# adaLN weights in one buffer of their own: blocks of 384 columns, eight k-tiles multiplied in one piece

## The chip, the cores and the metric

The kernel runs on one core of a Trainium2 chip. The metric is the device time of one execution in microseconds; smaller is better.

## The reference, cut to what matters

Two layers work on 256 context and 256 latent tokens of width 1024. Each layer first turns the two conditions into six modulation vectors of 1024 entries; two of them shift, two scale and two gate:

```python
mod_l = (silu_c @ ada_w[layer] + ada_b[layer])[:, None, :]
mod_c = (silu_cc @ ada_w[layer] + ada_b[layer])[None, None, :]
sh1_l, sc1_l, g1_l, sh2_l, sc2_l, g2_l = jnp.split(mod_l, 6, axis=-1)
...
h_l = rms_norm(xl, norm1_g[layer]) * (1.0 + sc1_l) + sh1_l
proj = jnp.concatenate([h_c, h_l], axis=1) @ w_in[layer]
...
xl = xl + g1_l * (jnp.concatenate([a_l, b_l, g_l], axis=-1) @ w_out[layer])
h2_l = rms_norm(xl, norm2_g[layer]) * (1.0 + sc2_l) + sh2_l
...
xl = xl + g2_l * y[:, y.shape[1] - n_lat:]
```

`proj` feeds three groups of heads (A: differential attention, B: windowed attention, C: gated linear attention). `y` is a SwiGLU in layer 0 (the FFN) and a choice of two out of eight experts in layer 1. `ada_w` is [2, 1024, 6144] in float32: per layer 48 blocks of 128 columns, eight blocks for each of the six vectors.

## The kernel before, in words

**Stages.** On TensorE the program runs: the projection of layer 0 with groups C, A and B; the output projection; the FFN in two halves of 1408 hidden columns; the same mixing for the latent tokens of layer 1; router and experts. Weights are loaded in float32 and split by ScalarE (high part, line 219) and VectorE (low part, line 385), and a product is three matmuls (lines 645 to 647).

**What sets the order.** Until the experts, all work is added as pieces to `Plan` (line 89): an engine, an estimated time, what it comes after, a rank, and the rings of buffers that it takes and gives back. `Plan.run` plays the list through once, on the host: whenever an engine is free, the first in rank of the pieces that can start goes next. What it finds is the order in which each engine's queue is written, DMA issues included; all the loads named here stand in SyncE's queue (SP). On the chip each queue runs strictly in that order.

**adaLN.** `ada` (line 421) makes one unit for `nb` blocks of 128 columns. It loads the columns of all eight k-tiles (line 431), into two halves or one buffer. `products` (line 442) multiplies four k-tiles at a time, each in its own 32 columns of the array, in two pieces of work; the second adds to the sums of the first. ScalarE copies the result (`adar`), TensorE transposes it block by block (`adat`, line 452), and VectorE adds the four rows and the bias into `mods` (lines 456 and 457). The buffer counts as free for the planner when the copy is done; on the chip the next load waits for the products alone.

**Where the units stand.** The first 16 blocks of layer 0 come at the start of the program, in buffers of the ring `long`. Blocks 16 to 41 are 13 units of two blocks in layer 0's attention, in the two buffers of the ring `raw`, through which all weights go as well. Blocks 42 to 47 and layer 1's blocks 0 to 31 are 13 units of three blocks (the last of two) in the FFN, in the two buffers `mixC`. Layer 1's blocks 32 to 47 are 8 units of two blocks in layer 1's attention, in `raw` again. The units of the attention have a rank behind everything else there: they fill.

**Around them.** Attention runs in units: scores (`sA`, `sB`, lines 1219 to 1221), exponentials (ScalarE, line 1231) on maxima by VectorE (line 1236), transposes (`pT`, line 1241), products with the values (`oAp`, `oBp`). The scores read `qmA`, the queries by groups in a tile that is zero elsewhere: GpSimd clears it (line 1190), ScalarE and VectorE write its high and low parts. `out_C` (weights `oCw`, line 1405) is group C's part of the output projection, in eight pieces of nine matmuls `oCp`; a piece needs its entry of the gate `g1`, and VectorE adds the result onto the tokens (line 653). It too fills the attention.

Of the kernel before, what the change touches and what calls it, by code (L numbers as in the profile page):

```python
# [11 lines left out]
F32 = mybir.dt.float32  # L12
# [7 lines left out]
PSUM = bass.MemoryType.PSUM  # L20
# [7 lines left out]
EPS = 1e-6  # L28
# [60 lines left out]
class Plan:  # L89
    """Pieces of work for the engines, issued in an order found by list scheduling: whenever an engine is free, the first  # L90
    in rank of the pieces whose needs are met and whose memory is free."""
# [8 lines left out]
    def add(self, engine, us, f, after=(), rank=0.0, take=(), give=(), order=()):  # L100
        """take, give: names of rings, a buffer each; taken at the start, given back at the end. order: names of
        sequences that the piece continues"""
# [6 lines left out]
    def release(self, after, rings):  # L109
        """gives memory back when the pieces are done"""  # L110
        return self.add("none", 0.0, lambda: None, after, 0.0, (), rings)
# [61 lines left out]
def trunk(ctx: ExitStack, tc: tile.TileContext, A, out, dbg=None):  # L173
    nc = tc.nc
# [23 lines left out]
    def acc4(n=4, kind=None):  # L198
        """accumulators of one product group: half of PSUM, one pair of banks and two single ones, or of one kind"""
# [25 lines left out]
    # ---------------- constants and small parameters  # L225
# [16 lines left out]
    # ---------------- tokens, feature-major  # L242
# [4 lines left out]
    def rsqrt_steps(get, scale, nm):  # L247
        """1 / sqrt(src * scale + EPS), with one Newton step, in pieces for DVE, ACT, DVE; get() returns dst, src"""
# [29 lines left out]
    plan = Plan(big=2, sm=4, hi=2, lo=2, raw=2, sp=2, work=10, long=24, mixC=2, b16=2, units=5, oC=2)  # L278
    add = plan.add

    # ---------------- tokens, feature-major, and the small parameters
# [9 lines left out]
    def start():  # L291
        """Returns the pieces after which silu(c), silu(c_ctx), the other small parameters and the tokens with their sums
        of squares are there."""
# [41 lines left out]
        # silu(c), silu(c_ctx) as the first two of 32 columns  # L335
# [38 lines left out]
    def parts(make, n, after, rank, take=(), give=(), order=()):  # L374
        """high and low parts of n columns; make() returns a list of (high, low, source). Returns the two pieces of work."""
# [14 lines left out]
    class Weights:  # L390
        """k-tiles of weights: load() returns the raw ones, views() the places of the high and low parts, pieces(self, k)
        a k-tile's (high, low, source)"""
# [21 lines left out]
    def w_load(src, segs, hk):  # L414
        """load of columns segs of src's k-tiles 4 hk .. 4 hk + 3, and its time"""
        return lambda: w_cols(src, segs, hk), 0.00146 * 4 * sum(n for _, n in segs)

    # ---------------- adaLN modulation, feature-major: mods[l][p, section*8 + k, (lat, ctx)]
    mods = [consts.tile([128, 48, 2], F32, name=f"mods{l}") for l in range(2)]

    def ada(l, b0, nb, rings, rank, after=()):
        """nb blocks of 128 columns from block b0 on; a column group of the array for each k-tile of four"""
# [4 lines left out]
        for i, r in enumerate(rings):  # L427
            def load(i=i, r=r):
                t = (KT(nm="idle") if r == "long" else k2.tile([128, 1536], F32, name="idle", tag=r, bufs=2) if r == "mixC" else
                     ring.tile([128, 2048], F32, name="idle", tag=r, bufs=2))[:, :per * n].rearrange("p (k f) -> p k f", k=per)  # L430
# [28 lines left out]
        a = add("PE", n * 0.002, lambda: products(0), [loads[(len(rings) - 1) // 2], have_c], rank, ["sm"])  # L459
        a = add("PE", n * 0.002, lambda: products(1), [a, *have], rank)  # L460
# [9 lines left out]
    def amul(l, sec, g, nm):  # L470
        """g * (1 + scale) of section sec, k-tiles lo..hi - 1 at a time."""
# [8 lines left out]
    def split(dst_hi, dst_lo, src, pieces=1):  # L480
        """pieces: along the first free dimension"""
# [7 lines left out]
    # ---------------- norm + modulation, feature-major  # L489

    def squares(k, t0, t1, after, rank, place=None):
        """squares of x^T's k-tile into the running sum (the last k-tile's stay apart); place: for the sum, where it outlasts
        this part"""
# [139 lines left out]
    def w_cols(src, segs, hk):  # L633
# [3 lines left out]
        o = 0  # L637
# [1728 lines left out]
```

## Time and profile before

| | |
|---|---|
| median of 3 runs | 1944.68 us (1943.29 to 1944.72) |
| profiled execution | span 1941.8 us; the page gives no other time of it |
| TensorE (PE) busy | 1904.0 us, 98% of the span |
| VectorE (DVE) busy | 1427.7 us, 74% |
| ScalarE (ACT) busy | 1170.6 us, 60% |
| adaLN products on PE | 57.1 us, 42 units |
| chain that ended last | PE 94%, DMA 2%, DVE 2%, ACT 1% |

Times in the trace count from the start of the span. A timeline row gives the start of its group, how long it was busy, engine, line, operation, output<-inputs, shapes and how many; in brackets the idle time of the engine just before it. Matmuls overlap, so the time that one takes from its engine is read from start to start. A float32 matmul of `adap` leaves two records. A window row gives for each engine its busy time and how many instructions, then the clock that was granted to PE (1.00 is 2.4 GHz), the busy share of the DMA engines, and GB/s.

### The profile page before, as it was taken

What the parts mean: (1) busy time and instruction counts of PE and PEld (TensorE: products, weight loads), DVE (VectorE), ACT (ScalarE), POOL (GpSimd) and SP (SyncE); (2) the same over time, 40 slices, a digit from 0 to 9 for tenths busy, and PEclk for the clock granted to TensorE, in tenths of its full rate; (3) what the DMA queues carried; (4) which work ended last, traced back from release to release, by engine and by line L of the source; (5) the groups of instructions that cost most, each with busy time, mean ns of one, the idle gap of its engine ahead of it and who ended that gap; (6) DMA issues with size and microseconds to landing.
All of it is one profiled execution on the core that took longest, in us unless ns stands there. A gap on an engine that the chain in (4) does not pass through costs nothing.

```text
span 1941.8 us, 27786 instructions
## 1 busy us (share of the span) xinstructions
PE 1904.0 (98%) x10317; PEld 1562.8 (80%) x10317; DVE 1427.7 (74%) x2330; ACT 1170.6 (60%) x1938; POOL 38.9 (2%) x44
## 2 busy tenths in 40 slices
PE   7999999999999999999999999999999999999998
PEld 4988678877787799887788888888888888888886
DVE  5564987433333345768889998999989999899997
ACT  4443684332222334448777777777777777777776
POOL 1001100000000000020000000000000000000000
PEclk9999999999999999999999999999999999999999
DMA  9313532435434423257799999999999999999991
GB/s 301 102 55 100 182 104 84 155 131 190 141 121 140 148 73 97 83 161 238 281 353 369 363 371 332 356 364 370 373 333 354 372 365 376 327 358 373 373 367 36
DMA packets 268911, 474.41 MB, mean 244 GB/s; under 512 B 14440, under 2 KB 75584, under 8 KB 268640
## 3 DMA queue, kind: packets, MB, share of 16 engines
q1 hardware_dynamic: 268384, 472.37, 69.6%
q8 instruction: 83, 1.36, 0.3%
q0 software_dynamic: 384, 0.19, 0.1%
q14 instruction: 60, 0.49, 0.1%
HBM read 471.47 MB, written 1.05 MB: 243 GB/s over the span
## 4 chain that ended last, share of the span: by engine, by line
PE 94%; DMA 2%; DVE 2%; ACT 1%; issue 0%; SPq 0%; DVEq 0%; ACTq 0%
PE gu L2110 32%; PE py L2135 16%; PE acc L645 9%; PE acc L647 8%; PE acc L646 8%; PE adap L442 2%; PE acc L855 2%; DMA idle<-in_ada_w 2%; PE acc L857 2%; PE acc L856 2%; PE pT L1241 1%; PE mtp L2124 1%; PE oBp L1329 1%; PE gth L2020 1%; PE sct L2159 1%; PE poC L1074 1%
## 5 line engine op out<-in xcount | busy, mean ns | idle before, releaser
L1845 DVE TENSOR_TENSOR mlo<-early,mhi 128x512 fp32r<-128x512 f32 (+1 forms) x350 | 340.0, 1019 | 24.6 <-issue 18.3
L219 ACT ACTIVATE mhi<-early 128x512 fp32r<-128x512 f32 (+1 forms) x352 | 291.3, 885 | 49.0 <-PE py L2135 25.1
L385 DVE TENSOR_TENSOR wlo<-raw,whi 128x512 fp32r<-128x512 f32 (+4 forms) x292 | 150.5, 564 | 157.8 <-ACT whi L219 157.0
L2110 PE MATMUL gu<-mlo,xh 128*128 128x512 f32 x896 | 247.9, 395 | 0.0
L219 ACT ACTIVATE whi<-raw 128x512 fp32r<-128x512 f32 (+4 forms) x292 | 134.9, 525 | 181.5 <-PE acc L646 146.5
L2110 PE MATMUL gu<-mhi,xh 128*128 128x512 f32 x896 | 244.0, 391 | 0.0
L2110 PE MATMUL gu<-mhi,xl 128*128 128x512 f32 x896 | 243.1, 390 | 0.0
L2135 PE MATMUL py<-mhi,hid 128*128 128x512 f32 x896 | 235.3, 390 | 0.0
L645 PE MATMUL acc<-hhi,whi 128*128 128x512 f32 (+1 forms) x576 | 217.6, 378 | 2.8 <-DVE rC L885 1.9
L646 PE MATMUL acc<-hlo,whi 128*128 128x512 f32 (+1 forms) x576 | 210.7, 366 | 2.2 <-DVE hlo L579 2.2
L647 PE MATMUL acc<-hhi,wlo 128*128 128x512 f32 (+1 forms) x576 | 210.6, 366 | 0.5 <-DVE wlo L385 0.5
L1845 DVE TENSOR_TENSOR mlo<-more,mhi 128x1024 fp32r<-128x1024 f32 (+1 forms) x174 | 198.5, 1184 | 11.9 <-issue 10.6
L2110 PEld LDWEIGHTS gu<-mhi,xl 128*128 128x128 f32 x896 | 168.2, 188 | 35.9
L2135 PEld LDWEIGHTS py<-mhi,hid 128*128 128x128 f32 x896 | 167.7, 188 | 35.6
L2110 PEld LDWEIGHTS gu<-mhi,xh 128*128 128x128 f32 x896 | 167.4, 188 | 34.4
L2110 PEld LDWEIGHTS gu<-mlo,xh 128*128 128x128 f32 x896 | 164.4, 188 | 31.5
L219 ACT ACTIVATE mhi<-more 128x1024 fp32r<-128x1024 f32 (+1 forms) x174 | 169.0, 1022 | 28.2 <-PE py L2135 28.2
L1845 DVE TENSOR_TENSOR mlo<-mraw,mhi 128x1024 fp32r<-128x1024 f32 (+1 forms) x116 | 132.5, 1186 | 15.6 <-ACT mhi L219 8.5
L1845 DVE TENSOR_TENSOR mlo<-spare,mhi 128x1024 fp32r<-128x1024 f32 x108 | 127.3, 1220 | 15.3 <-PE py L2135 8.0
L645 PEld LDWEIGHTS acc<-hhi,whi 128*128 128x128 f32 x576 | 108.8, 189 | 35.3 <-issue 11.2
L646 PEld LDWEIGHTS acc<-hlo,whi 128*128 128x128 f32 x576 | 108.9, 189 | 18.9 <-DVE hlo L579 3.1
L647 PEld LDWEIGHTS acc<-hhi,wlo 128*128 128x128 f32 x576 | 108.7, 189 | 18.7 <-DVE wlo L385 0.9
(371 smaller groups left out, 3035.2 us busy)
## 6 DMA issues: line engine op xcount, KB each, us to landing
early<-in_moe_w_up SPq DMA_DIRECT2D x56, 1024.0 KB, 6.0
more<-in_moe_w_up SPq DMA_DIRECT2D x54, 1024.0 KB, 6.2
early<-in_moe_w_gate SPq DMA_DIRECT2D x52, 1024.0 KB, 6.5
spare<-in_moe_w_down SPq DMA_DIRECT2D x48, 1024.0 KB, 6.0
early<-in_moe_w_down SPq DMA_DIRECT2D x112, 256.0 KB, 6.1
mraw<-in_moe_w_gate SPq DMA_DIRECT2D x27, 1024.0 KB, 6.2
mraw<-in_moe_w_down SPq DMA_DIRECT2D x27, 1024.0 KB, 5.7
more<-in_moe_w_gate SPq DMA_DIRECT2D x24, 1024.0 KB, 6.3
```

What stands on the lines that cost most here:

```text
L219: act(o, i, AF.Copy)
L385: tt(l_, v, h, op=OP.subtract)
L442: mm(w["pm"][32 * g:32 * g + 32, :n], sil[:, 4 * i + g, :], w["raw"][4 * i + g], start=i == 0, stop=i == 1, tile_position=(0, 32 * g))
L645: mm(o, lh, rh, start=start, stop=False)
L646: mm(o, lh, rl, start=False, stop=False)
L647: mm(o, ll, rh, start=False, stop=stop)
L855: mm(p, t["hi"][:, kk, s], w.w[0][:, k, :], start=kk == 0, stop=False)
L856: mm(p, t["hi"][:, kk, s], w.w[1][:, k, :], start=False, stop=False)
L857: mm(p, t["lo"][:, kk, s], w.w[0][:, k, :], start=False, stop=kk == KD - 1)
L1845: tt(l, w, h, op=OP.subtract)
L2110: mm(out, a[kk // 2][:, kk % 2, o:o + 128], b[:, k, :], start=i + kk == 0, stop=i == 2 and kk == KD - 1)
L2135: mm(out, a[:, k, :], b[:, k, :], start=i + c + k == 0, stop=i == 2 and c == NCH - 1 and k == 3)
```

## The change

`ada` takes one buffer `adw` of 12 KB per partition where it took two halves in other rings; the planner knows one such buffer. With one buffer all eight k-tiles are one piece of work. All units behind layer 0's first 16 blocks have three blocks (layer 0's last one two) and form one chain of loads: 11 of layer 0 with the old rank, and 16 of layer 1 with ranks that spread them over the FFN. Layer 1's attention has none left. The room comes from a tile that was never used, `wm`, and from the scratch of the DMA descriptors that GpSimd writes (4096 bytes now).

```diff
-    plan = Plan(big=2, sm=4, ..., units=5, oC=2)
+    plan = Plan(big=2, sm=4, ..., units=5, oC=2, adw=1)
...
             def load(i=i, r=r):
-                t = (KT(nm="idle") if r == "long" else k2.tile([128, 1536], F32, name="idle", tag=r, bufs=2) if r == "mixC" else
-                     ring.tile([128, 2048], F32, name="idle", tag=r, bufs=2))[:, :per * n].rearrange("p (k f) -> p k f", k=per)
+                t = (KT(nm="idle") if r == "long" else k2.tile([128, 3072], F32, name="adw", tag=r, bufs=1))[:, :per * n]
+                t = t.rearrange("p (k f) -> p k f", k=per)
...
-        a = add("PE", n * 0.002, lambda: products(0), [loads[(len(rings) - 1) // 2], have_c], rank, ["sm"])
-        a = add("PE", n * 0.002, lambda: products(1), [a, *have], rank)
+        if len(rings) == 1:
+            a = add("PE", 0.65 + n * 0.004, lambda: [products(i) for i in range(2)], [*have, have_c], rank, ["sm"])
+        else:
+            a = add("PE", n * 0.002, lambda: products(0), [loads[(len(rings) - 1) // 2], have_c], rank, ["sm"])
+            a = add("PE", n * 0.002, lambda: products(1), [a, *have], rank)
...
-    wm = K2((128, 256), nm="wm")
...
-        for b in range(EARLY if last else 16, 48 if last else 42, 2):
-            ada(l, b, 2, ["raw"], base + FILL + b, [wB[1].loaded])
+        if not last:
+            x = [wB[1].loaded]
+            for b in range(16, 48, 3):
+                x = ada(0, b, min(3, 48 - b), ["adw"], base + FILL + b, x)
+            ranks = [6000 + 1000 * g + v for g in range(2) for v in (12, 62, 112, 162, 212, 262, 412, 512)]
+            for b in range(0, 48, 3):
+                x = ada(1, b, 3, ["adw"], ranks[b // 3], x)
...
-        fill = [(0, b, min(3, 48 - b)) for b in range(42, 48, 3)] + [(1, b, min(3, EARLY - b)) for b in range(0, EARLY, 3)]
...
-                for x in range(2):
-                    if fill:
-                        ada(*fill.pop(0), ["mixC", "mixC"], R + 12 + x, read[-1:])
...
-    nc = bacc.Bacc("TRN2", target_bir_lowering=False, num_devices=1)
+    nc = bacc.Bacc("TRN2", target_bir_lowering=False, num_devices=1, dynamic_dma_scratch_size=4096)
```

**How it moves instructions.** Lines of the change stand one to three higher than before. Place 1 is PE's queue at the start of layer 0's attention. Before, nine matmuls of `out_C` stand between the transposes of the second unit and the first scores:

```order
L452 MATMUL adat<-cst,adar 128x128 x2
L645 MATMUL oCp<-mixC,oCh 128x512
L646 MATMUL oCp<-mixC,oCh 128x512
L647 MATMUL oCp<-mixC,oCl 128x512
L645 MATMUL oCp<-mixC,oCh 128x512
L646 MATMUL oCp<-mixC,oCh 128x512
L647 MATMUL oCp<-mixC,oCl 128x512
L645 MATMUL oCp<-mixC,oCh 128x512
L646 MATMUL oCp<-mixC,oCh 128x512
L647 MATMUL oCp<-mixC,oCl 128x512
L1219 MATMUL sA<-thi,qmA 128x256
L1220 MATMUL sA<-tlo,qmA 128x256
```

With the change, from the first unit on:

```order
L442 MATMUL adap<-adw,sil 32x384 x8
L1158 MATMUL rp<-kB_1910,cst_80 128x256
L1158 MATMUL rp<-qB_1906,cst_80 128x256
L452 MATMUL adat<-cst,adar 128x128 x3
L1887 MATMUL ppt<-cst,prow 128x8
L1220 MATMUL sA<-thi,qmA 128x256
L1221 MATMUL sA<-tlo,qmA 128x256
```

The second unit and the nine matmuls of `out_C` have moved behind the first scores.

Place 2 is SP's queue in layer 0's attention, the loads by which the units are fed. Before:

```order
L1405 DMA oCw<-in_w_out 128x3x256
L431 DMA idle<-in_ada_w 128x8x256
L1405 DMA oCw<-in_w_out 128x3x256
L431 DMA idle<-in_ada_w 128x8x256 x6
L1405 DMA oCw<-in_w_out 128x3x256
L431 DMA idle<-in_ada_w 128x8x256 x6
L1512 DMA raw<-in_w_out 128x2x1024
```

With the change:

```order
L1406 DMA oCw<-in_w_out 128x3x256 x2
L1518 DMA raw<-in_w_out 128x2x1024
L1406 DMA oCw<-in_w_out 128x3x256
L1524 DMA raw<-in_w_out 64x3x512 x2
L431 DMA adw<-in_ada_w 128x8x384 x6
L1406 DMA oCw<-in_w_out 128x3x256
L431 DMA adw<-in_ada_w 128x8x384 x3
L1524 DMA raw<-in_w_out 64x3x512 x2
```

The first load of the output projection's weights has moved ahead of the adaLN loads, all but one of which now stand behind a load of the same buffer.

Place 3 is PE's queue ahead of layer 1's attention. Before:

```order
L442 MATMUL adap<-idle,sil 32x256 x8
L1157 MATMUL rp<-qB_7807,cst_80 128x256
L1157 MATMUL rp<-kB_7811,cst_80 128x256
L452 MATMUL adat<-cst,adar 128x128 x2
L442 MATMUL adap<-idle,sil 32x256 x8
L645 MATMUL oCp<-mixC,oCh 128x256
L646 MATMUL oCp<-mixC,oCh 128x256
L647 MATMUL oCp<-mixC,oCl 128x256
```

With the change:

```order
L648 MATMUL oCp<-mixC,oCh 128x256
L649 MATMUL oCp<-mixC,oCh 128x256
L650 MATMUL oCp<-mixC,oCl 128x256
L1158 MATMUL rp<-qB_7812,cst_80 128x256
L648 MATMUL oCp<-mixC,oCh 128x256
L649 MATMUL oCp<-mixC,oCh 128x256
L650 MATMUL oCp<-mixC,oCl 128x256
L1158 MATMUL rp<-kB_7819,cst_80 128x256
```

The units are gone, and matmuls of `out_C` have moved up: 27 of its 72 stand ahead of the first scores (18 before), and the other 45 inside the attention.

## Rows read from the trace of the kernel before

**Rows 1.** Busy time by stage: window, length, PE, PEld, DVE, ACT, POOL, clock, DMA.

```profile
192.80:247.00 54.20, 50.86 (x433) 35.36 (x433) 46.88 (x132) 38.72 (x111) 10.40 (x4) 1.00 0.58 185
247.00:300.00 53.00, 53.00 (x468) 40.30 (x467) 43.56 (x145) 39.97 (x124) 1.75 (x1) 1.00 0.31 88
330.00:742.00 412.00, 409.25 (x2190) 330.63 (x2191) 161.92 (x340) 129.35 (x258) 0.41 (x2) 1.00 0.40 133
854.80:915.00 60.20, 59.92 (x536) 43.60 (x537) 51.88 (x153) 48.10 (x131) 12.28 (x4) 1.00 0.76 247
951.70:1941.80 990.10, 977.92 (x4472) 808.25 (x4471) 903.09 (x950) 751.75 (x909) 0.00 (x0) 1.00 0.95 343
```

**Rows 2.** The same view for tile `adap` alone: PE, PEld, ACT, clock, DMA.

```profile
192.80:300.00 107.20, 14.70 (x208) 4.97 (x208) 4.80 (x13) 1.00 0.45 137
330.00:742.00 412.00, 21.12 (x208) 4.40 (x208) 6.25 (x13) 1.00 0.40 133
854.80:915.00 60.20, 8.77 (x128) 3.25 (x128) 2.90 (x8) 1.00 0.76 247
```

**Rows 3.** Timeline of PE around four pieces of adaLN work.

```profile
203.59 1.07 PE L442 MATMUL adap<-idle,sil 128*32 128x256 f32 x16 [0.75 <-DMA idle<-in_ada_w]
204.59 0.50 PE L645 MATMUL oCp<-mixC,oCh 128*128 128x512 f32 x1
...
383.10 0.39 PE L647 MATMUL acc<-hhi,wlo 128*128 128x512 f32 x1
383.42 0.85 PE L442 MATMUL adap<-idle,sil 128*32 128x384 f32 x8
...
384.54 0.39 PE L646 MATMUL acc<-hlo,whi 128*128 128x512 f32 x1
384.77 0.39 PE L647 MATMUL acc<-hhi,wlo 128*128 128x512 f32 x1
...
476.96 0.39 PE L647 MATMUL acc<-fhh,wlo 128*128 128x512 f32 x1
477.19 0.49 PE L452 MATMUL adat<-cst,adar 128*128 128x128 f32 x3
...
477.75 0.40 PE L646 MATMUL acc<-fhl,whi 128*128 128x512 f32 x1
...
531.10 1.50 PE L442 MATMUL adap<-idle,sil 128*32 128x384 f32 x16
...
532.86 0.40 PE L646 MATMUL acc<-hlo,whi 128*128 128x512 f32 x1
```

**Rows 4.** Tile `mods`: ns min/median/max, first and last start in us.

```profile
L456 DVE TENSOR_REDUCE mods<-adat x42: 153/174/183, 17.7 to 911.2; 128x4 f32<-128x16 f32 x30, 128x6 f32<-128x24 f32 x12
L457 DVE TENSOR_TENSOR mods<-mods,ppar x42: 161/164/167, 17.9 to 911.4; 128x4 f32<-128x4 f32 x30, 128x6 f32<-128x6 f32 x12
```

**Rows 5.** Timelines of POOL, DVE and PE at the start of layer 0's attention.

```profile
192.66 6.97 POOL L1190 MEMSET qmA<- 128x4096 f32 x2 [37.85 <-PE acc L646]
...
197.51 2.82 DVE L385 TENSOR_TENSOR qmA<-qA,qmA 32x512 fp32r<-32x512 f32 x4
...
199.03 0.28 PE L1219 MATMUL sA<-thi,qmA 128*128 128x256 f32 x1
```

**Rows 6.** As rows 1, two short windows of layer 1.

```profile
790.00:795.00 5.00, 3.09 (x15) 2.63 (x15) 4.78 (x13) 2.95 (x6) 0.00 (x0) 0.91 0.00 0
795.00:800.00 5.00, 5.00 (x28) 4.19 (x28) 4.25 (x14) 1.94 (x7) 0.00 (x0) 0.75 0.52 153
```

**Rows 7.** Loads of `ada_w`: issues, us to landing, PE's wait for them.

```profile
idle<-in_ada_w SPq DMA_DIRECT2D x24, 768.0 KB, 6.2
...
DMA to landing us min/median/max: 3.9/6.5/9.4
...
PE adap L442 <- DMA idle<-in_ada_w: 3.2, 2, 2.4
```

More of the change, by code (lines that the diff above doesn't have):

```diff
@@ L276, in rsqrt @@
         newton()
-    plan = Plan(big=2, sm=4, hi=2, lo=2, raw=2, sp=2, work=10, long=24, mixC=2, b16=2, units=5, oC=2)
+    plan = Plan(big=2, sm=4, hi=2, lo=2, raw=2, sp=2, work=10, long=24, mixC=2, b16=2, units=5, oC=2, adw=1)
     add = plan.add
@@ L810, in trunk @@
     FILL = 5000
-    EARLY = 32
     def mixing(l, base, t, tiles, wC, started=None):
@@ L1717, in ffn @@
                                     sums[x].append(q)
-                if fill:
-                    ada(*fill.pop(0), ["mixC", "mixC"], R + 12, read[-1:])
             plan.release(used, ["long"] * 22)
```

## The prediction

> **What bounds the kernel now.** I began with the busy time by stage [rows 1]. Its reader should set the length of each window beside PE's busy time: 50.86 of 54.2 us and 53.00 of 53 in the two halves of layer 0's attention, 409.25 of 412 in the FFN, 59.92 of 60.2 in layer 1's attention, 977.92 of 990.1 in the experts. PE is the bound nearly everywhere, so a microsecond of PE work is in general a microsecond of time. The second thing to see is VectorE: 46.88 of 54.2, 43.56 of 53 and 51.88 of 60.2 in the attention (shares of 0.865, 0.82 and 0.86), but only 161.92 of 412 in the FFN. In the attention, then, PE is busy partly because adaLN units and `out_C` fill the time in which the chain of scores, maxima, exponentials and transposes waits for VectorE. Removing fill there does not give all of its time back. In the FFN nothing waits for another engine, and each piece added costs its full time.
>
> Second, the units. `adap` has 208, 208 and 128 records in layer 0's attention, the FFN and layer 1's attention [rows 2]; at 16 per unit that is 13, 13 and 8. Third, the timeline of PE, for prices [rows 3].
>
> **Prices.** Undisturbed matmuls of 512 columns start every 0.23 us (384.54 to 384.77). A half of 384 columns: from the matmul ahead of it (383.10) to the one behind (384.54) are 1.44 us; one of the three matmuls behind has no record (line 647 is followed by 646), so two steps of 0.23 come off: 0.98. A whole 384: 532.86 − 531.10 = 1.76, less 0.23 for the record missing there too, plus the 0.09 by which the half started late (383.42 − 383.10 − 0.23): 1.62. Two halves are 1.96, so the whole saves 0.34. A whole 256: 204.59 − 203.59 = 1.00, plus 0.09 ahead and the 0.11 by which the matmul behind it is long (0.50 against 0.39): 1.20; halved, by the same 0.34, 1.54. The transposes of three blocks: 477.75 − 476.96 = 0.79 less two steps = 0.33; of two blocks two thirds, 0.22. So a new unit of three blocks is 1.95, of two 1.42. On VectorE a unit costs 0.17 + 0.16 us whatever its blocks [rows 4], 0.34 with rounding. ScalarE copies once per unit, 4.80 / 13 = 0.37 to 0.48 us [rows 2], and is never the fuller engine [rows 1]: nothing.
>
> **PE's ledger, part by part.** (How many units were halved is counted on the timeline.)
> - Layer 0's attention: before, nine whole and four halved units of two blocks, 9 × 1.20 + 4 × 1.54 + 13 × 0.22 = 19.8; now ten units of three and one of two, 10 × 1.95 + 1.42 = 20.9. +1.1.
> - FFN: before, ten halved and two whole units of three blocks and one of two, 19.6 + 3.24 + 1.20 + 12 × 0.33 + 0.22 = 28.2; now sixteen of three (one of them just ahead of it), 31.2. +3.0.
> - Layer 1's attention: before, six whole and two halved, 7.2 + 3.08 + 1.76 = 12.1; now none. −12.1.
>
> The sum is −8.0 on PE. What becomes of it in time differs by stage.
>
> **FFN: +3.0.** PE has no idle time there to take it (2.75 us in 412), and VectorE is at 0.39.
>
> **Layer 1's attention: −6.1.** PE's work falls to 59.92 − 12.1 = 47.8, VectorE's to 51.88 − 8 × 0.34 = 49.2. VectorE becomes the fuller engine. Nearest row for how full it can be when it is nearly the bound: the experts, 903.09 of 990.1, 0.91. 49.2 / 0.91 = 54.1 against 60.2: −6.1. Bounds: −11.0 if VectorE were never idle (49.2), −3.1 if it stays at its present 0.86 (57.1). The `out_C` that moves up fills holes ahead of the scores and leaves as much room behind: nothing, at most 1 us either way.
>
> **Layer 0's attention: +3.8.** The units are chained now and spread later: by the order, five in place of ten stand ahead of the first scores of B (the first half, about 192.8 to 247), and 24 in place of 30 matmuls `oCp`. First half: PE 50.86 − (15.6 − 9.75) − 6 × 0.23 = 43.6, VectorE 46.88 − 5 × 0.34 = 45.2. VectorE would set the pace: 45.2 / 0.91 = 49.7, −4.5 (bounds −9 with no idle time, −1.9 at 0.865). Second half, where PE has no idle time at all: the rest of the ledger, 1.1 + 5.85, and 1.4 of `oCp`: +8.3. Together +3.8.
>
> **The first scores: +0.6.** Ahead of them PE loses its cover: nine `oCp` (2.07) and the second unit (1.42), 3.5 us, less some 0.5 for the larger first unit; PE would be there 3 us sooner. But the scores read `qmA`, which POOL begins to clear at 192.66 (two in 6.97 us) and whose low parts VectorE writes from 197.51, four in 2.82; the first is done at about 198.2, and the scores began at 199.03 [rows 5]. So PE will stand idle some 2.6 us. That idle time is already in the share used above; what may come on top is the clock. In layer 1 PE idled 1.91 of the 5 us from 790, at a granted clock of 0.91, and the next 5 us had 0.75 [rows 6]: half of them at 1.2 in place of 2.4 GHz, 1.25 us of work lost. I take half of that, +0.6; the bounds are 0 and 1.3.
>
> **Loads and queues.** SP's queue gets one DMA of 1.5 MB where two of 768 KB stood. All the units' loads but the first now wait for the products of the unit ahead, and `oCw`, `w_out` and in the FFN the weights stand behind them. A pair of 768 KB took 6.2 us in the median, 9.4 at worst, and PE waited for `ada_w` twice, 3.2 us in all [rows 7]. In the first half units would follow each other every 49.7 / 5 = 9.9 us, in the second every 61.3 / 6 = 10.2. Product and load make 1.42 + 6.2 = 7.6: covered, and the 3.2 us of waits I leave as they are, since the weights that now go ahead free the ring `raw` no sooner. In the FFN the DMA engines are busy 0.40 of the time [rows 1], and the planner's ranks spread sixteen loads over 412 us. The unused tile and the descriptors' scratch stand in no PE wait: POOL's share in DMAs is off the chain, nothing (without that cover the cost would show as POOL's wait ahead of its next transfer).
>
> **A rule against the change.** The rows say that 7.6 us of cycle fit into 9.9. The Trainium skill, in "Trainium Kernel Development and Optimization", section Best Practices, asks to double-buffer so that transfers run beside compute; one buffer gives that up for these loads. By the rule each unit would pay for its load; by the rows the load has 2.3 us to spare. The rival that follows from rows alone is the next part's first.
>
> **Sum.** +3.8 + 3.0 − 6.1 + 0.6 = +1.3. The profiled span is 1941.8, the median of the runs 1944.68; the 2.9 around the span stays. 1944.7 + 1.3 = **1946.0 us**. A measurement of this kernel can tell about 0.2%, 3.9 us, from no change.
>
> **The rivals.**
> 1. *One buffer starves PE (slower).* PE stands at a unit in its strict order until the load lands. It decides from a landing of 9.9 − 1.42 = 8.5 us on. With the longest one seen, 9.4, the cycle is 10.8: 0.9 × 5 + 0.6 × 6, some 8 us more with the two halves, 1946 + 8 = 1954. For: the load is twice as large as one DMA before. Against: two waits of 42 units before, and a DMA share of 0.58 and 0.31 in the attention. Chance 0.14.
> 2. *PE sets the pace everywhere (faster).* VectorE packs more tightly once PE is less full, and idle time stays as it was: the ledger's −8.0, 1936.7. For: PE's share of 0.94 to 1.00. Against: VectorE's 49.2 of 52 us in layer 1 would be 0.95, more than any stage shows. Chance 0.23.
> 3. *VectorE gets no fuller (slower).* It stays at 0.865 and 0.86: first half −1.9, layer 1 −3.1, so 2.6 and 3.0 worse than the sum: +6.9, 1951.6. For: these are the shares of the very stages, and taking away fill does not shorten a chain of maxima and exponentials. Against: the fill itself stood in that chain on PE. Chance 0.15.
> 4. *The change doesn't do what it says.* Its loads on SP, each waiting for products of PE, hold the FFN's weights back behind them, so that the FFN pays more than its ledger. Against: a DMA share of 0.40 there. Chance 0.03, some 1955.
>
> **How the numbers follow.** The forecast itself has 0.45: its bounds (layer 1 from −11 to −3, the first half from −9 to −2, the clock 0 to 1.3) make 1940 to 1950. To 0.8 it must reach towards rivals 2 and 3: 1938 to 1953. Faster by over 0.2% (under 1940.8): nearly all of rival 2 and a small part of the forecast, 0.24. Slower by over 0.2% (over 1948.6): rivals 1, 3 and 4 and little of the forecast, 0.33. Within: 0.43.
>
> **What the profile would show.** Right: `adap` in pieces of eight pairs at about 1.6 us, 16 of them in the FFN and none from 840 to 925; the FFN 3 us longer; layer 1's attention near 54 us with PE at 0.88 and VectorE at 0.91; PE idle 2 to 3 us ahead of the first scores, waiting for `qmA`. Rival 1: PE's waits for `adw` far over 3.2 us. Rival 2: PE still at 0.99 in layer 1's attention. Rival 3: VectorE at 0.86 there. I am wrong altogether if layer 0's attention grows by much more than 4 us, since its ledger has only +1.1, or if the FFN, the surest term, grows by something other than 3.

## The result and the profile after

The changed kernel took 1956.70 us in the median, the kernel before 1943.99 on the same chip: slower, ratio 1.0068 with a 95% interval of 1.0052 to 1.0084, some 12.7 us. (In one of its four runs the granted clock stood at 0.556 throughout; without that run the median is 1956.03, 12.0 above, so differences that start from 12.7 carry this 0.7.) The prediction said 1946.0, with a range of 1938 to 1953. The profiled execution has a span of 1953.9 us, 12.1 more than that of before.

Where the 12.1 us went is read from four milestones on PE's timeline that both kernels have. Of the kernel before: the norm's sums ahead of the FFN, the first product behind layer 1's norm, layer 1's first scores, the router:

```profile
323.34 0.28 PE L547 MATMUL nst<-ones,ssq 128*128 128x1 f32 x2
...
735.46 0.36 PE L645 MATMUL acc<-hhi,whi 128*128 128x256 f32 x1
...
860.62 0.39 PE L1219 MATMUL sA<-thi,qmA 128*128 128x512 f32 x1
...
939.39 0.81 PE L1966 MATMUL lgp<-h,rt 128*8 128x256 f32 x3 [1.11 <-ACT h L566]
```

And of the changed one:

```profile
333.06 0.28 PE L550 MATMUL nst<-ones,ssq 128*128 128x1 f32 x2
...
748.01 0.37 PE L648 MATMUL acc<-hhi,whi 128*128 128x256 f32 x1
...
870.32 0.39 PE L1220 MATMUL sA<-thi,qmA 128*128 128x512 f32 x1
...
950.82 3.62 PE L1966 MATMUL lgp<-h,rt 128*8 128x256 f32 x16 [1.11 <-ACT h L569]
```

The differences: +9.7 by the end of layer 0's mixing, +2.8 in the FFN, −2.9 from there to layer 1's first scores, +1.7 from those scores to the router, and +0.7 behind it. The prediction had +4.4, +3.0 and, for all of layer 1, −6.1. The second milestone isn't sharp: other products of layer 1 stand ahead of it, 54 matmuls before and 66 now, 1.4 us more. Counted up to the first of these (727.76 and 738.87), the differences are +1.4 in the FFN and −1.4 from there to the first scores.

By place, layer 0's +9.7 is: first scores 2.2 earlier, +1.5 from there to the first scores of B, some +3.1 to the last scores, and some +7.3 behind them. In that last stretch now stand three units and 42 matmuls of `out_C`, where before there were no products of units and 33 matmuls.

The windows that answer to [rows 1], set this time by the scores themselves: group A and group B of layer 0, and the first 20 us of layer 1's scores. First the kernel before (columns as in rows 1):

```profile
199.00:247.60 48.60, 45.67 (x388) 31.97 (x387) 43.29 (x119) 34.61 (x104) 4.80 (x3) 1.00 0.58 183
247.60:284.50 36.90, 36.90 (x342) 27.68 (x340) 30.07 (x111) 28.94 (x95) 1.15 (x1) 1.00 0.33 100
...
854.80:860.60 5.80, 5.80 (x59) 4.24 (x59) 3.55 (x13) 3.47 (x9) 5.80 (x2) 1.00 0.62 198
860.60:880.60 20.00, 19.72 (x166) 13.26 (x165) 19.10 (x47) 15.71 (x42) 4.67 (x2) 1.00 0.74 231
```

Then the changed kernel, the same places:

```profile
196.80:246.90 50.10, 45.15 (x324) 31.71 (x324) 44.76 (x115) 35.70 (x101) 8.11 (x3) 0.97 0.46 154
246.90:286.90 40.00, 39.05 (x359) 28.93 (x359) 30.47 (x113) 30.48 (x99) 0.00 (x0) 1.00 0.41 129
...
870.30:890.30 20.00, 16.83 (x111) 13.28 (x110) 18.84 (x42) 14.67 (x38) 4.78 (x2) 1.00 0.36 126
870.30:950.80 80.50, 70.87 (x555) 59.00 (x553) 63.86 (x170) 55.86 (x147) 6.79 (x4) 0.98 0.40 133
```

Look at VectorE in the 20 us windows: 19.10 us before, 18.84 after. It was nearly full already. The short window ahead of the scores, 854.80 to 860.60, is where VectorE had only 3.55 of 5.80 us: the window of [rows 1] had mixed the two into 0.86.

The rest of layer 1 falls into three stretches: first scores of A to first scores of B, from there to the last scores, from there to the router. Before, then after:

```profile
860.62:885.79 25.17, 24.89 (x208) 17.40 (x206) 23.61 (x56) 20.08 (x54) 5.35 (x3) 1.00 0.80 253
885.79:903.38 17.59, 17.59 (x142) 12.49 (x142) 16.27 (x56) 14.42 (x42) 1.11 (x1) 1.00 0.66 241
903.38:939.39 36.01, 34.26 (x326) 31.43 (x324) 27.33 (x74) 24.19 (x61) 0.20 (x1) 1.00 0.66 199
...
870.32:895.56 25.24, 22.07 (x143) 17.81 (x142) 24.00 (x53) 18.62 (x49) 5.30 (x3) 1.00 0.29 100
895.56:914.84 19.28, 19.28 (x163) 14.58 (x161) 16.31 (x54) 16.42 (x49) 1.27 (x1) 1.00 0.30 108
914.84:950.82 35.98, 29.50 (x254) 26.60 (x253) 23.55 (x64) 20.82 (x52) 0.20 (x1) 0.95 0.54 171
```

In the first stretch PE lost 2.8 us of work and nothing got shorter; VectorE has 0.94 and 0.95 of it. In the second PE is full in both kernels, and it got 1.7 longer: nine matmuls of `out_C` stand in it now. In the third PE lost 4.8 us, since `out_C` moved up (tile `oCp` there: 45 matmuls before, 3 after), and again nothing got shorter.

What filled the third stretch is a wait. ScalarE, which takes its queue strictly in order, stood 3.06 us at `wh` for a load, and the three `whi` that PE needed stood behind it:

```profile
928.36 1.15 ACT L219 ACTIVATE wh<-raw 128x512 fp32r<-128x512 f32 x2 [3.06 <-DMA raw<-in_w_out]
...
929.57 1.66 ACT L219 ACTIVATE whi<-raw 128x512 fp32r<-128x512 f32 x3
...
930.24 0.39 PE L648 MATMUL acc<-mBh,whi 128*128 128x256 f32 x1 [2.80 <-ACT whi L219]
```

The units themselves, as in [rows 2] (tile `adap`: PE, PEld, ACT, clock, DMA): eleven in layer 0, sixteen in the FFN, none in layer 1's attention. So the change does what it says.

```profile
192.70:340.00 147.30, 17.75 (x184) 4.99 (x188) 5.30 (x11) 0.99 0.45 144
340.00:742.00 402.00, 23.55 (x256) 6.46 (x248) 7.66 (x16) 1.00 0.43 144
870.30:950.80 80.50, 0.00 (x0) 0.00 (x0) 0.00 (x0) 0.98 0.40 133
```

What PE waited for between 180 and 340 us (us in total, times, longest); the list before had its longest entry at 1.5, 0.8 and 0.7:

```profile
PE adat L452 <- ACT adar L219: 1.6, 1, 1.6
PE pT L1242 <- DVE unit L1282: 1.6, 2, 1.4
PE sA L1220 <- ACT qmA L219: 1.1, 1, 1.1
PE adap L442 <- DMA adw<-in_ada_w: 1.1, 1, 1.1
PE pT L1242 <- DVE mx L1274: 0.9, 1, 0.9
PE sB L1220 <- ACT unit L1232: 0.8, 1, 0.8
```

No single wait is large; there are more of them. Summed over PE's timeline from 180 us to the norm, the idle time in brackets is 8.3 us, before 3.3. And from 180 us on the granted clock fell at two places after PE had been idle: behind the first scores (waits of 1.1 and 0.4 us for `qmA`, then 1.1 for `adw`), and behind the wait of 2.80 us at 930.24 for the weights of layer 1's output projection.

```profile
200.00:205.00 5.00, 3.95 (x23) 1.63 (x24) 4.75 (x12) 4.55 (x13) 0.00 (x0) 0.66 0.10 33
930.00:935.00 5.00, 4.34 (x20) 3.95 (x21) 2.92 (x6) 1.75 (x4) 0.00 (x0) 0.66 0.29 66
```

A clock of 0.66 over 5 us is 1.7 us of PE's work lost each time. The kernel before had one such place there, 0.09 + 0.25 of 5 us [rows 6], also 1.7, behind a wait of 1.91 us. The changed kernel has that wait too, and its clock stayed up:

```profile
803.37 0.50 PE L648 MATMUL acc<-hhi,whi 128*128 128x512 f32 x1 [1.90 <-DVE rC L886]
...
800.00:805.00 5.00, 3.10 (x20) 2.61 (x19) 4.71 (x13) 3.74 (x8) 0.00 (x0) 1.00 0.00 0
```

### The profile page after: what moved, and what is told of

It reads as the page before. It is cut to its first block, busy times and chain, and to the rows that moved or that the text cites. A ratio compares the mean times of both kernels' runs of the same rounds, so it can differ in the third digit from the quotient of the medians.

```text
span 1953.9 us, 27518 instructions
## 1 busy us (share of the span) xinstructions
PE 1901.4 (97%) x10205; PEld 1563.2 (80%) x10205; DVE 1425.8 (73%) x2316; ACT 1169.8 (60%) x1931; POOL 38.9 (2%) x44
## 4 chain that ended last, share of the span: by engine, by line
PE 91%; DVE 3%; DMA 3%; ACT 2%; issue 0%; SPq 0%; DVEq 0%; ACTq 0%
PE gu L2110 31%; PE py L2135 16%; PE acc L648 9%; PE acc L649 9%; PE acc L650 9%; PE acc L856 2%; PE acc L858 2%; PE acc L857 2%; PE adap L442 2%; PE mtp L2124 1%; DMA idle<-in_ada_w 1%; PE pT L1242 1%; PE gth L2020 1%; PE sct L2159 1%; DVE mx L1237 1%; PE poC L1075 1%
## 5 line engine op out<-in xcount | busy, mean ns | idle before, releaser
L1845 DVE TENSOR_TENSOR mlo<-early,mhi 128x512 fp32r<-128x512 f32 (+1 forms) x350 | 340.0, 1019 | 25.2 <-issue 17.7
L1845 DVE TENSOR_TENSOR mlo<-mraw,mhi 128x1024 fp32r<-128x1024 f32 (+1 forms) x116 | 132.5, 1186 | 15.3 <-ACT mhi L219 8.5
```

What stands on the lines that cost most here:

```text
L1845: tt(l, w, h, op=OP.subtract)
```

## The experiments

All against runs of the kernel before on the same chip; the last column is the difference of the two medians.

| run | median us | ratio, 95% interval | us to before |
|---|---|---|---|
| the change | 1956.70 | 1.0068 (1.0052 to 1.0084) | +12.7 |
| l1_back | 1945.64 | 1.0014 (1.0005 to 1.0023) | +2.2 |
| l0_back | 1952.93 | 1.0044 (1.0030 to 1.0058) | +9.4 |
| both_back | 1941.65 | 0.9988 (0.9979 to 0.9997) | −1.8 |
| no_l1 | 1945.73 | 1.0011 (1.0002 to 1.0020) | +2.2 |
| no_l0 | 1934.46 | 0.9966 (0.9952 to 0.9980) | −8.3 |
| dve_more | 1963.28 | 1.0110 (1.0095 to 1.0126) | +20.5 |
| act_more | 1956.40 | 1.0075 (1.0062 to 1.0089) | +13.7 |
| price_129 | 1950.04 | 1.0036 (1.0022 to 1.0051) | +7.1 |
| price (1.62) | 1949.33 | 1.0038 (1.0024 to 1.0052) | +6.6 |
| price_189 | 1954.95 | 1.0062 (1.0045 to 1.0079) | +12.0 |
| price_254 | 1961.85 | 1.0102 (1.0085 to 1.0118) | +18.9 |
| cover | 1957.78 | 1.0073 (1.0059 to 1.0086) | +14.7 |
| later | 1958.35 | 1.0076 (1.0063 to 1.0090) | +15.3 |
| price_l1 | 1939.30 | 0.9978 (0.9969 to 0.9987) | −3.8 |
| price_both | 1939.64 | 0.9982 (0.9973 to 0.9991) | −3.4 |
| price_l1_24 | 1946.52 | 1.0018 (1.0009 to 1.0027) | +3.5 |

### Each part undone alone, and both

Theory 1: VectorE sets the pace in the attention, so units there are free, and units in the FFN cost their full time. Theory 2: PE's ledger holds everywhere. The run l1_back (the units that go back are loaded into `raw` and multiplied in two pieces, with prices as before; those lines are not shown):

```diff
-            for b in range(0, 48, 3):
-                x = ada(1, b, 3, ["adw"], ranks[b // 3], x)
+            for b in range(0, 32, 3):
+                x = ada(1, b, min(3, 32 - b), ["adw"], ranks[b // 3], x)
+        else:
+            for b in range(32, 48, 2):
+                ada(1, b, 2, ["raw"], base + FILL + b, [wB[1].loaded])
```

> The changed kernel with one part undone: layer 1's blocks 32 to 47 go back into layer 1's attention as eight units of two blocks in the ring raw; the FFN keeps eleven units of the new kind in place of sixteen. Theory 1 (VectorE's chain sets the pace in the attention, so a unit there is free, and one in the FFN costs its full 1.95 us): the FFN gets 31.2 - 20.9 = 10.3 us shorter, layer 1's attention stays within 1 us of the changed kernel's: 1956.7 - 10 = about 1946.5. Theory 2 (PE's ledger holds everywhere): 10.3 us off the FFN, 12.1 us onto layer 1: about 1958.5.

The run l0_back:

```diff
-            for b in range(16, 48, 3):
-                x = ada(0, b, min(3, 48 - b), ["adw"], base + FILL + b, x)
+            for b in range(16, 42, 2):
+                ada(0, b, 2, ["raw"], base + FILL + b, [wB[1].loaded])
+            x = [wB[1].loaded]
+            for b in range(42, 48, 3):
+                x = ada(0, b, 3, ["adw"], 6002 + b / 10, x)
```

> The changed kernel with the other part undone: layer 0's blocks 16 to 41 go back into layer 0's attention as thirteen units of two blocks in the ring raw; blocks 42 to 47 become two units of the new kind at the start of the FFN. Theory 1 (units in the holes of the attention are free, what the change pushed behind the last scores was paid in full): the 9.7 us that the changed kernel has lost by the norm ahead of the FFN come back, the two units in the FFN cost 3.9: 1956.7 - 5.8 = about 1951. Theory 2 (PE's ledger): layer 0's units cost 19.8 in place of 20.9, the two in the FFN 3.9 on top: 1956.7 + 2.8 = about 1959.5.

> Both parts undone, so that only the new buffer and the product in one piece are left, in the FFN's units: places as in the kernel before, thirteen units in the FFN, ten of which were halved before. Theory 1 and theory 2 both give 10 x 0.34 = 3.4 us less than the kernel before, about 1940.6, if a whole piece is 0.34 us cheaper than two halves. A third theory (the one buffer itself costs, by loads that come late or that hold back others on SP's queue): at or above 1944.

With layer 1 undone the time fell by 10.5 us (12.7 to 2.2), as theory 1 had it; theory 2 had wanted a rise. In its trace the FFN, up to the first product of layer 1, is 10.4 shorter than in the changed kernel, where the ledger has 10.3. With layer 0 undone it fell by 3.3 where theory 1 had 5.8 and theory 2 a rise of 2.8: right in sign, short in size. With both undone, and only the buffer and the whole piece left in the FFN, the kernel is 1.8 us faster than before: less than 3.4, but the third theory, that the one buffer costs by itself, falls for the units of the FFN.

### Left out where they stood

In no_l1 the eight units of layer 1's attention are left out of the kernel before, in no_l0 the thirteen of layer 0's; the blocks hold the bias alone.

```diff
-        for b in range(EARLY if last else 16, 48 if last else 42, 2):
-            ada(l, b, 2, ["raw"], base + FILL + b, [wB[1].loaded])
+        for b in () if last else range(16, 42, 2):
+            ada(l, b, 2, ["raw"], base + FILL + b, [wB[1].loaded])
+        if last:
+            def bias():
+                nc.vector.tensor_copy(mods[1][:, 32:48, :], adab[1][:, 32:48][:, :, None].to_broadcast([128, 16, 2]))
+
+            a = add("DVE", 0.3, bias, [wB[1].loaded, have_small], base + 100)
+            for b in range(32, 48):
+                mod[l, b] = a
```

> The kernel before without the eight units of layer 1's attention: their loads, products, copies, transposes and sums are left out, and blocks 32 to 47 of layer 1 are the bias alone, written by one VectorE instruction. It measures what these units cost where they stood. Theory 1 (free, VectorE sets the pace): within 2 us of the kernel before. Theory 2 (PE's ledger): 12.1 us less, about 1932. The prediction's own middle course: 6 us less, about 1938.

> The kernel before without the thirteen units of layer 0's attention: their loads, products, copies, transposes and sums are left out, and blocks 16 to 41 of layer 0 are the bias alone. It measures what these units cost where they stood. Theory 1, for the part ahead of B's first scores only, where VectorE is at 0.9: the ten units there are free, the three in the second half, where PE had no idle time, cost 1.42 each: some 4 us less, 1939.5. PE's ledger: 19.8 less, about 1924.

Without 12.1 us of PE's work the kernel is not faster but 2.2 us slower. The windows of no_l1, the first 20 us from the first scores, all from there to the router, and the part behind the last scores:

```profile
858.10:878.10 20.00, 16.86 (x111) 13.29 (x110) 18.86 (x42) 14.64 (x38) 4.77 (x2) 1.00 0.37 126
858.10:938.50 80.40, 70.68 (x555) 58.94 (x553) 63.78 (x170) 55.81 (x147) 6.78 (x4) 0.98 0.41 133
...
902.41:938.54 36.13, 29.51 (x255) 26.59 (x253) 23.55 (x64) 20.81 (x52) 0.20 (x1) 0.95 0.54 170
```

They are those of the changed kernel almost to the digit: 80.40 us against 80.50, VectorE at 18.86 of 20. So on balance the units of layer 1's attention had cost nothing. This doesn't mean that nothing could be gained: behind the last scores no_l1 too has some 4.8 us less of PE's work and the same length, with a wait of 2.9 us for `whi` and the clock at 0.95. Layer 0's thirteen cost 8.3 us where PE's ledger has 19.8; I had expected 4, so more than the three in the second half were paid. Some 6.3 of the 8.3 came behind the last scores (39.1 to 32.8 us), where 33 matmuls of `out_C` had stood and none do in no_l0.

### Is it VectorE?

That PE isn't the pace doesn't show that VectorE is. dve_more repeats the maxima of four units of group A in layer 1, act_more the first exponentials of eight, both in the changed kernel (a line that lets act_more's repeat write the same tile is not shown).

```diff
-            a = add("DVE", 0.06 + 1.07 * x, lambda: highest(u), [a], rank)
+            twice = 2 if last and i < 8 and i % 2 == 0 else 1
+            a = add("DVE", twice * (0.06 + 1.07 * x), lambda: [highest(u) for _ in range(twice)], [a], rank)
```

> The changed kernel with more VectorE work in layer 1's attention: four of the eight units of group A take their maxima twice (the same 128x1024 reduction again, some 1.1 us each, 4.5 us in all; the planner is told). PE and ScalarE do what they did. Theory 1 (VectorE sets the pace there): 3 to 5 us more than the changed kernel's 1956.7. A rival (the chain's latency or PE sets the pace, VectorE has 0.1 of the time to spare): under 1 us more.

```diff
-            a = add("ACT", 0.24 + 0.42 * x, lambda: exps(u, 0, scale), [b, pairs.get(i // 2)], rank,
+            twice = 2 if last and i < 8 else 1
+            a = add("ACT", twice * (0.24 + 0.42 * x), lambda: [exps(u, 0, scale) for _ in range(twice)], [b, pairs.get(i // 2)], rank,
```

> The changed kernel with more ScalarE work in the same place: each of the eight units of group A computes its first exponentials twice (the same instruction again, some 0.65 us each, 5.2 us in all; the planner is told). Theory 1 (VectorE alone sets the pace): within 1.5 us of the changed kernel's 1956.7. A rival (the chain through ScalarE is as tight, or its latency counts): 3 to 6 us more.

From the first scores of A to those of B, where the repeats stand, and from the last scores to the router, dve_more:

```profile
869.14:904.82 35.68, 26.41 (x149) 21.57 (x148) 30.40 (x63) 19.07 (x50) 6.56 (x3) 0.86 0.20 71
...
924.24:954.92 30.68, 26.98 (x247) 24.37 (x245) 22.40 (x60) 21.08 (x53) 0.20 (x1) 1.00 0.64 198
```

act_more:

```profile
872.26:901.32 29.06, 25.02 (x155) 20.64 (x154) 25.99 (x57) 23.76 (x64) 5.70 (x3) 0.94 0.25 87
...
921.02:951.71 30.69, 27.00 (x247) 24.37 (x245) 22.39 (x60) 21.10 (x53) 0.21 (x1) 1.00 0.62 198
```

In the medians VectorE's extra work costs 7.8 us and ScalarE's 1.0, which looks as if only VectorE counted. The stretches say otherwise. In both runs the part behind the last scores is 5.3 us shorter than in the changed kernel (30.7 for 35.98), because the planner, told of the longer pieces, wrote another order: the three `whi` now stand ahead of `wh` in ScalarE's queue, and PE waits 0.9 us there.

```profile
931.83 1.66 ACT L219 ACTIVATE whi<-raw 128x512 fp32r<-128x512 f32 x3
...
935.77 1.68 ACT L219 ACTIVATE wh<-raw 128x512 fp32r<-128x512 f32 x3 [2.28 <-DMA raw<-in_w_out]
```

(These two rows are of act_more.) Where the repeats stand, 5.26 us more of VectorE made the stretch 10.4 longer (25.24 to 35.68), and 5.56 more of ScalarE made it 3.8 longer (to 29.06). The granted clock, 0.86 and 0.94 there, accounts for at most 5.0 and 1.7 of these. So VectorE's work is paid at least in full, and ScalarE's in part: some 2 us or more. The chain of maxima and exponentials sets the pace in group A, and VectorE is the fuller of its two engines; that VectorE alone sets it isn't shown. Both runs also change the planner's order, which no run here separates from the work itself.

### The planner's price

What made layer 0 lose more than its ledger? The planner prices the whole piece at 0.65 + 0.004 per column, 2.19 us for 384; the trace has 1.62. In the planner's picture PE is then busy where on the chip it waits, and `out_C` isn't put there. One number is changed:

```diff
-            a = add("PE", 0.65 + n * 0.004, lambda: [products(i) for i in range(2)], [*have, have_c], rank, ["sm"])
+            a = add("PE", 0.08 + n * 0.004, lambda: [products(i) for i in range(2)], [*have, have_c], rank, ["sm"])
```

> The changed kernel with one number changed: the planner prices the product in one piece at 0.08 + 0.004 per column, 1.62 us for 384 columns as the trace has it, in place of 0.65 + 0.004, 2.19. Six matmuls of out_C go back ahead of layer 0's first scores. If the first scores' lost cover and the clock behind it cost 2 to 3 us, they come back: about 1954. If that place costs nothing: 1956 to 1957. If the planner's wrong price is behind the units that stand behind layer 0's last scores too: 1950 or less.

It gave back 6.1 us, half of the whole loss (7.4 if the two medians are compared without their own runs of the kernel before, as later expectations do). In the trace the norm ahead of the FFN stands at 328.39 (changed kernel: 333.06), so 4.7 of it lie in layer 0: 3.4 between the first and the last scores of B, 1.5 behind them. PE's idle time up to the norm is 5.2 us (8.3), and the clock behind the first scores stays up:

```profile
200.00:205.00 5.00, 4.88 (x36) 2.96 (x35) 4.81 (x11) 4.74 (x13) 0.00 (x0) 1.00 0.33 64
```

I then tried to find the place by hand, with the wrong price kept: in cover, six matmuls of `out_C` ahead of the first scores; in later, the second unit moved behind the third unit of attention as well.

```diff
+        if not last:
+            plan.ops[units[0]["Sop"]][3].append(done["outC", 0, 1])
+            plan.ops[mod["product", 0, 19]][3].append(units[0]["Sop"])
```

(In later the last line names `units[2]`; "Sop" is a unit's scores, "product" a unit's piece.)

> The changed kernel with one place mended and the planner's price as it was: the first scores of layer 0 are made to come after the first six matmuls of out_C, and the second unit after the first scores, as with the right price. If PE's idle time ahead of the first scores and the low clock behind it (0.66 of 5 us) are what the wrong price cost in layer 0's attention: 3 to 4 us less than the changed kernel, about 1953, and no low clock at 200 to 205. If the wrong price costs through the later places: 1956 to 1957.

> The changed kernel with the wrong price kept and two places set by hand: the first scores come after six matmuls of out_C, and the second unit after the scores of the third unit of attention; twelve more matmuls of out_C then stand ahead of it. In the run before this one the second unit still stood where its load had not landed (PE waited 1.01 us for adw, then 3.44 us for exponentials that it had held up, and the clock fell to 0.72). If that place is what the wrong price cost in layer 0: no wait for adw, no low clock at 200 to 215, 4 to 5 us less than the changed kernel, about 1952. If the cost lies in the later units: 1956 to 1958.

Both failed: +14.7 and +15.3 us where the change has +12.7. PE stood idle at other places. In cover it waited for the second unit's load and then for exponentials:

```profile
201.40 1.50 PE L442 MATMUL adap<-adw,sil 128*32 128x384 f32 x16 [1.01 <-DMA adw<-in_ada_w]
...
206.34 0.39 PE L1220 MATMUL sA<-thi,qmA 128*128 128x256 f32 x1 [3.44 <-ACT unit L1232]
...
205.00:210.00 5.00, 3.66 (x17) 3.27 (x18) 3.48 (x13) 3.62 (x14) 0.00 (x0) 0.72 0.84 296
```

In later the load was there, and the wait for exponentials stayed:

```profile
207.69 0.58 PE L1220 MATMUL sA<-thi,qmA 128*128 128x256 f32 x1 [3.19 <-ACT unit L1232]
...
205.00:210.00 5.00, 2.31 (x11) 2.31 (x12) 4.92 (x17) 2.34 (x9) 0.00 (x0) 0.68 0.00 0
```

So setting the first scores' cover and the second unit's place by hand brings nothing back; since the planner then orders all that follows anew, this doesn't say what each place costs by itself. Is it chance, then, which order comes out? Three more prices:

> The changed kernel with the planner's price of a whole piece of 384 columns at 1.29 us, less than the 1.62 of the trace (0.004 per column less 0.25). If the right price is what counts: worse than with 1.62 (1949.3), 1950 to 1953. If a low price is good in itself, because it spares cover for the real queue: at or under 1949. If the order is a lottery: anything from 1948 to 1958.

> The same with 1.89 us, half way between the right price and the changed kernel's 2.19. No matmul of out_C stands ahead of the first scores, as with 2.19. If the error of the price is paid in proportion: about 1953. If it is paid through the first scores' cover: about 1956.

> The same with 2.54 us, further off than the changed kernel's 2.19. If the error of the price is paid in proportion: about 1960. If 2.19 was a chance hit of a bad order: 1949 to 1955.

| price of 384 columns, us | 1.29 | 1.62 | 1.89 | 2.19 | 2.54 |
|---|---|---|---|---|---|
| us to the kernel before | +7.1 | +6.6 | +12.0 | +12.7 | +18.9 |
| norm ahead of the FFN, us | 328.39 | 328.39 | 331.60 | 333.06 | 336.73 |
| PE idle from 180 to it, us | 4.2 | 5.2 | 5.4 | 8.3 | 8.7 |

Five orders are few, but they don't look like a lottery: the one price that is too low costs nothing that can be told, and of those too high 2.54 costs more than 1.89 and 2.19, which can't be told apart. Through which single places it is paid stays open. The planner's price of the load was wrong too, 4.5 us (8 x 384 x 0.00146) where it landed in 7.1; no run changed that one.

### Together

price_l1 has the right price and layer 1's blocks 32 to 47 back in its attention; price_both has layer 0's part undone as well; price_l1_24 puts blocks 24 to 47 into layer 1's attention (`range(24, 48, 2)` in place of `range(32, 48, 2)`).

> The right price of the product in one piece, and layer 1's blocks 32 to 47 back in layer 1's attention as pairs. If the two gains add up (7.4 by the price, 11.1 by layer 1): 1956.7 - 18.5 = about 1938, some 5 us less than the kernel before. If the price only mends what the units of layer 1 in the FFN had disturbed: about 1945.6.

> Both parts undone and the right price; the new buffer serves the FFN's thirteen units alone. Theory 1: the price matters only where units stand in layer 0's attention, so this stays within 2 us of the run with both parts undone, 1941.7, and the right price with layer 0's part kept is as good or better.

> As the run with the right price and layer 1's blocks 32 to 47 in its attention, but with blocks 24 to 47 there: twelve pairs in place of eight, and eight units in the FFN in place of eleven. It asks where the free room in layer 1's attention ends. If all twelve are free: 5.3 us less (the FFN's 20.9 to 15.6), about 1933. If the room ends at eight (PE was busy 59.92 of 60.2 us there before): four more pairs cost 1.42 to 1.76 each, 5.7 to 7, so about 1938.5 to 1940.

price_l1 is 3.8 us faster than the kernel before, ratio 0.9978 (0.9969 to 0.9987), the best here together with price_both, from which it can't be told apart. With the right price the new buffer can stay in layer 0. Twelve pairs were too many: 7 us more than eight, and some 6 more than the expectation's worse case. In the trace the last four stand behind the last scores, PE waits 2.98 us for the output projection's weights, which had to follow them through the ring `raw`, and the clock fell to 0.50 from 920 to 925. The room in layer 1's attention ends between eight pairs and twelve.

## Why the prediction was wrong

- **Layer 1, −6.1: this step failed, at two of its terms.** The first is VectorE's share. The prediction took 0.86 as the present share and 0.91 as the one to be reached, and gave the difference to the change. The window began six microseconds ahead of the scores, where VectorE had 3.55 of 5.80 us; from the first scores to the last it had 39.88 of 42.76, 0.93, and 0.955 in the first 20 us. There was nothing to gain: group A's stretch took 25.2 us with the units, without them (no_l1) and with the change. The second term is `out_C`, put at "nothing, at most 1 us either way". Its move took most of 4.8 us of PE's work out of the stretch behind the last scores, and none of it came back, as PE then waited 2.80 us for `whi` and the clock fell. With the other order of dve_more and act_more that stretch is 5.3 us shorter. So some 5 us could have been gained in layer 1, at a place where the prediction had none. That the order in ScalarE's queue kept them back is read from the traces; no run changes it alone.
- **Ahead of layer 1's scores, −2.9 (or −1.4 by the sharper milestone).** The two units that stood there are worth 2 × 1.42. Another 1.7 is the low clock of [rows 6], which the changed kernel happens not to have behind the same wait: that part is luck. What `out_C` and new waits (1.4 us for `oCl`) add goes the other way.
- **Layer 0, +4.4 with the clock: this step failed in size.** 9.7 were measured, which the prediction itself had named as a sign of being wrong. The first half's −4.5 rested on the same window error: 43.29 of 48.60 from the first scores on is 0.89, so the ceiling of 0.91 was all but reached. The first half took 50.1 us from first scores to first scores of B, 1.5 more than before, with fewer units in it. The loss splits, on PE's timeline, into some 5.0 us more idle time, 3.4 more for `adap` and its transposes (1.1 of it foreseen, 1.3 at half clock: 2.79 for a piece of 1.50), and 1.8 more in `sA`. With the right price (run price) layer 0 lost 5.1, close to the 4.4, but that nearness is luck: the first half was 1.1 longer, not 4.5 shorter.
- **The price in the planner** stands in the change's own diff, beside 1.62 in my price list. I didn't set the one against the other; it was worth 6.1 us.
- **FFN, +3.0: right in kind.** 2.8 measured, or 1.4 by the sharper milestone; the units there are paid in full, as l1_back shows.
- **The first scores: right in kind.** PE idled for `qmA` (1.1 and 0.4), then for `adw` (1.1), and the clock fell to 0.66, 1.7 us where I had taken 0.6 with a bound of 1.3. Which of these waits brought the clock down isn't shown.
- **Rival 1, the one buffer starving PE,** had the sign and nearly the time (1954), and was not the mechanism: PE waited once for `adw`, 1.1 us, in 27 loads, though the landing was 7.1 us rather than 6.2. The Trainium skill ("Trainium Kernel Development and Optimization", Best Practices) asks for two buffers. Here the trace does not bear it out as a direct cost, but for that wait and its share in the low clock behind it: it stands where the first two units came 8.6 us apart, and a load and a product take 8.7; from then on the units of the first half came every 11 to 12 us. Whether two buffers of 384 columns would have kept the last units ahead of the last scores wasn't tried.
- **Rival 3** (VectorE gets no fuller, 1951.6, chance 0.15) named what happened in group A of layer 1: taking away fill did not shorten the chain. It still gave back 3.1 us there that didn't come. **Rival 2** had PE's ledger: for the attention, l1_back, no_l1 and no_l0 all speak against it. The prediction's argument against it, that 0.95 on VectorE was more than any stage shows, held for the averages only.
- **Slips that decide nothing.** Layer 1's ledger adds up to 12.04, not 12.1; and the cycle of product and load took 1.42, the price of a whole unit of two blocks, where a product of 384 columns has 1.62.

## What to carry to other kernels

Ask of each stretch which engine is full in it, from the first instruction of its real work to the last; a window that begins a few microseconds early hides a full engine. Work that fills another engine's shadow can be free there (eight units in layer 1's attention were, on balance) and is paid in full where nothing else is waited for, as in the FFN. Read an added or a left-out piece of work in the stretch where it stands, and look at the others for what a new order did: the sum from first scores to router hid +3.8 and −5.3. And when pieces are regrouped, the planner's price of the new piece is part of the change: too high a price leaves holes that the planner can't see.

## What was not expected of the hardware

A stall of PE can cost twice, but it need not. In nearly every kernel here the granted clock fell at some places behind idle times of about 1.4 to 3.6 us, to 0.66 or 0.75 over 5 us most often, about 1.7 us of work each time. The same wait of 1.9 us ahead of layer 1's attention (for `rC`) stands in all 18 kernels: behind it the clock fell in 8 profiled executions, the kernel before among them, and stayed up in 10, the changed kernel among them. A wait of 3.0 us left it up too (no_l1, at 43 us). So 1.7 us at one such place are no sign of what a change did. The Trainium skill ("TensorE: Matmul & The Clock Gate", HAM oscillation) tells of waits for DMA that throttle the engine; the rows agree in kind, show it behind waits for other engines too, and even an engine that is busy 97% of the span pays for them. And a single load of 1.5 MB took 7.1 us to land, where two of 768 KB issued together had 6.2 [rows 7]:

```profile
adw<-in_ada_w SPq DMA_DIRECT2D x26, 1536.0 KB, 7.1
```
